# Hybrid S5 and sparse-attention block: factors of B ahead of the last tables, octet 0's rotation products behind the next weights, the second sweep's spills on SyncE

## The chip, the cores and the metric

One core of one Trainium2 chip. The time is that of one execution on the device in microseconds (us); before the change it is 2343.06, the median of 3 runs (2338.4 to 2365.14). The engines are TensorE (PE), VectorE (DVE), ScalarE (ACT), GpSimd (POOL) and SyncE (SP). Each executes its own instructions in the order of its queue; a transfer (DMA) is issued by an engine, here SP or POOL, and carried by the 16 transfer engines of the core.

## The reference

A decoder block on x (1, 512, 2048). An adaLN-modulated RMSNorm feeds one combined projection; its output goes to a diagonal complex state-space group (S5, 64 groups of 16 channels with 64 states) and to sparse attention, whose keys and values are some of the projection's columns. A convolutional gated MLP follows.

```python
h = modulate(rmsnorm(x, g_mix_norm[l]), sh1, sc1)
u, q, kc, vc, ks, vs, kw, vw, gl = jnp.split(h @ w_in[l], split_at, axis=-1)
...
den = lr * lr + li * li                    # in s5_mixer
f_re = (num_re * lr + ab_im * li) / den
f_im = (ab_im * lr - num_re * li) / den
bb_re = f_re[..., None] * br - f_im[..., None] * bi
bu = lax.complex(jnp.einsum('bsgh,gph->sbgp', uf, bb_re), jnp.einsum('bsgh,gph->sbgp', uf, bb_im))
_, states = lax.associative_scan(_lin_rec_combine, (a, bu), axis=0)
y = (einsum(real(states), c_re) - einsum(imag(states), c_im) + d_skip * uf)
```

## The kernel before, in words

**Precision.** Each float32 operand of a large product is split in two: ACT rounds a copy (`..h`), DVE subtracts it from the source (`..l`; `split`, L72 to L78, which a profile shows as L75). A product is three matmuls of 128x128 on 128x512 (`mm3`, L100 to L102); only the third reads the low half of the weight.

**Phase a** (`phase_a`, L211) runs twice over the 16 blocks of D. The second sweep fills eight PSUM banks: four heads of keys `pk[0..3]`, four blocks of values. At its end the first bank is rotated (`rope`), each is split into a buffer `adw` and written to DRAM, keys to `qk_d` (`spill`, L675, two halves of 512 rows, 512 KB each), values to `v_d` (L319, 256 KB each), for the attention later. All eight transfers are issued by POOL.

**S5 tables** (`s5_prep`, L339) are made by POOL at low priority during phase a: powers of the state matrix (PR, PI), a table of rotations in two factors (CA, SA and CB, SB; from CA, SA the copies CH, SH), and the factors of B, `s5fr` and `s5fi` (fr, fi), one of whose inputs is a reciprocal on DVE (L441). It is a generator, called at the start and the end of the first sweep. Its last stage normalises both tables (L485 to L491).

**Phase b1** (`phase_b1`, L677) has 12 projections of 48 matmuls. `weights` (L80) loads 1 MB (`wr`, two buffers, SP) and splits it in two halves (`wh`, `wl`, two buffers each). Projection 0 is followed by a rope on DVE (L708 to L710, `qt`, `qr`), whose tables `rt` (a tile of name `sp`) SP loads at L685. Between the projections stand the eight octets of S5 (`s5_octet`, L508). On DVE an octet forms `s5bb` = B with fr and fi (L526 to L532), `s5bg` from it (L542 to L544, transposed by PE at L585), `s5TT` (L547), the six rotation products `s5C`, `s5S` (L563 to L569; C and S are later copied and scaled by ACT), and, later, the bias row `s5wt` (L610), which reads `shb`, a broadcast of the shift, loaded behind the values' spills by POOL (L689). The block matrix goes out to `k_s` and back into the single buffer `s5w3` (shown as `s5w`, L603). The tiles of the octets lie in memory that phase a's buffers, `adw` among them, held.

**Order.** The code is in program order; a scheduler at build time orders each engine's queue by its estimates of when operands are ready, and by priority (`tc.high_priority`, with a negative number for late). `self.after(parts, x)` keeps instructions behind x, on the engine's queue or by a wait; `Held(V, f)` is an engine that does so with each instruction that it is given.

Of the kernel before, what the change touches and what calls it, by code (L numbers as in the profile page):

```python
# [10 lines left out]
F32 = mybir.dt.float32  # L11
# [3 lines left out]
ALU = mybir.AluOpType  # L15
# [3 lines left out]
P = 128  # L19
D = 2048  # L20
# [44 lines left out]
class Block:  # L65
    def __init__(self, ctx, tc, a):
        self.ctx, self.tc, self.a = ctx, tc, a
        self.nc = tc.nc
        self.V, self.A, self.T = tc.nc.vector, tc.nc.scalar, tc.nc.tensor


    def split(self, src, hi, lo, scale=None):  # L72
# [7 lines left out]
    def weights(self, src, out=None, first=None):  # L80

        res = []
        with self.tc.high_priority():
            raw = self.wp.tile([P, 2048], F32, name="wr", bufs=2)
            self.nc.sync.dma_start(raw, src)
            for h in range(2):
                if out is None:
                    hi = self.wp.tile([P, 8, P], F32R, name="wh", bufs=2)
                    lo = self.wp.tile([P, 8, P], F32R, name="wl", bufs=2)
                else:  # L90
                    hi, lo = out[:, 2 * h], out[:, 2 * h + 1]
                parts = self.split(raw[:, 1024 * h:1024 * h + 1024].rearrange("p (k m) -> p k m", m=P), hi, lo)
                if first is not None:
                    self.after(parts, first)
                res.append((hi, lo))
        return res

# [113 lines left out]
    def phase_a(self, hh, hl, tab, ps):  # L211


        nc, tc, a, V, A, T = self.nc, self.tc, self.a, self.V, self.A, self.T
        m, b = self.mod, self.mad
        with ExitStack() as st:
            pa = st.enter_context(tc.tile_pool(name="pa", bufs=1))
            pw = st.enter_context(tc.tile_pool(name="pw", bufs=1, side="right"))
            xq = [pa.tile([P, 4, S], F32, name=f"x{q}") for q in range(4)]
            xt = [xq[k // 4][:, k % 4] for k in range(KT)]  # L220
            rb = pa.tile([P, S], F32, name="rb")
# [54 lines left out]
            for kt in range(KT):  # L276
# [3 lines left out]
                V.tensor_add(m[:, 0, kt:kt + 1], ash, b[:, 0, kt:kt + 1])  # L280
                if kt >= 8:
                    hl[kt] = tab.tile([P, S], F32R, name=f"hl{kt}")
                self.modulate(xt[kt], m[:, 1, kt:kt + 1], m[:, 0, kt:kt + 1], rb, hh[kt], hl[kt], pa)
                if kt < 8:
                    V.tensor_mul(us[kt], us[kt], rp)
                if kt == 4:
# [20 lines left out]
            for i in range(4):  # L307
                p = pk[i]
                if i == 0:
                    q, t = (pa.tile([P, 8, 64], F32, name="modt", bufs=2).rearrange("p a b -> p (a b)")  # L310
                            for _ in range(2))
                    p = self.rope(p, q, t, self.rot[:, 0], self.rot[:, 1], 64)
                if i % 2 == 0:
                    o = tmp(4).bitcast(F32R)
                self.spill(self.qk_d[0, P * i:P * i + P], p, o[:, 2 * (i % 2):2 * (i % 2) + 2])
            o = tmp(4)
            for t in range(4):
                A.copy(o[:, t], pk[4 + t])
                self.v_spill = nc.gpsimd.dma_start(self.v_d[t], o[:, t])  # L319

    def modulate(self, x, gain, shift, rb, hi, lo, pool, t=None):
        if t is None:
# [16 lines left out]
    def s5_prep(self, pool, W):  # L339
# [4 lines left out]
        with tc.high_priority(-100000):  # L344
            n = [0]

            def t(shape=(P, 64), dt=F32, name=None):
                n[0] += 1
                return W.tile(list(shape), dt, name=name or f"sp{n[0]}")
# [83 lines left out]
        with tc.high_priority(-100000):  # L433
# [4 lines left out]
            V.tensor_mul(den, lr, lr)  # L438
            V.tensor_mul(q, li, li)
            V.tensor_add(den, den, q)  # L440
            self.V.reciprocal(rd, den)  # L441
            V.tensor_scalar(nr, ar, -1.0, None, op0=ALU.add)
            fr = pool.tile([P, 64], F32, name="s5fr")
            fi = pool.tile([P, 64], F32, name="s5fi")
            V.tensor_mul(fr, nr, lr)
            V.tensor_mul(q, ai, li)
            V.tensor_add(fr, fr, q)
            V.tensor_mul(fr, fr, rd)
            V.tensor_mul(fi, ai, lr)
            V.tensor_mul(q, nr, li)  # L450
            V.tensor_sub(fi, fi, q)
            V.tensor_mul(fi, fi, rd)
            V.tensor_scalar(fi, fi, sgn, None, op0=ALU.mult)
            r8 = pool.tile([P, 64], F32, name="s5r8")
            V.tensor_mul(r8, mag, mag)
            V.tensor_mul(r8, r8, r8)
# [25 lines left out]
            cmul(fc, fs, ec, es, ec, es, tmp[:, 0])  # L482
            powers(CA, SA, fc, fs)
            n1 = t((P, 8, 64))
            for C, Sn in ((CB, SB), (CA, SA)):  # L485

                V.tensor_mul(n1, C, C)
                V.tensor_mul(tmp, Sn, Sn)
                V.tensor_add(n1, n1, tmp)
                V.tensor_scalar(n1, n1, -0.5, 1.5, op0=ALU.mult, op1=ALU.add)  # L490
                V.tensor_mul(C, C, n1)  # L491
                V.tensor_mul(Sn, Sn, n1)
                V.tensor_scalar(Sn, Sn, sgn, None, op0=ALU.mult)
# [14 lines left out]
    def s5_octet(self, o, Tb, W, ps):  # L508
# [49 lines left out]
            return tab[:, :, G].rearrange("p b g -> p g b").unsqueeze(2).to_broadcast([P, 8, 4, 8])  # L558


        Ch, Sh = C[:, :, 0:4], Sn[:, :, 0:4]
        tc1 = W.tile([P, 8, 8, 8], F32, name="s5x", bufs=4)[:, :, 0:4]
        V.tensor_mul(Ch, ab(Tb["CH"]), ba(Tb["CB"]))  # L563
# [3 lines left out]
        V.tensor_mul(Sh, ab(Tb["SH"]), ba(Tb["CB"]))  # L567
        V.tensor_mul(tc2, ab(Tb["CH"]), ba(Tb["SB"]))
        V.tensor_add(Sh, Sh, tc2)  # L569
        for x, sg in ((C, 1.0), (Sn, -1.0)):  # L570
            A.activation(x[0:64, :, 4:8], x[64:P, :, 0:4], AF.Copy, scale=sg)
            A.copy(x[64:P, :, 4:8], x[64:P, :, 0:4])
            A.activation(x[64:P, :, 0:4], x[0:64, :, 0:4], AF.Copy, scale=sg)
# [96 lines left out]
        V.tensor_add(q, q, t)  # L670
        return q

    def spill(self, dst, q, t, scale=None):
        self.split(q, t[:, 0], t[:, 1], scale)
        self.nc.gpsimd.dma_start(dst, t.bitcast(F32))  # L675

    def phase_b1(self, hh, hl):  # L677
        nc, tc, a, V, A, T = self.nc, self.tc, self.a, self.V, self.A, self.T
        with ExitStack() as st:
# [6 lines left out]

            nc.sync.dma_start(self.sh_d.rearrange("o (p k) -> (o p) k", k=KT), self.mod[:, 0])
            shb = self.shb = W.tile([P, D], F32, name="shb")
            self.after([nc.gpsimd.dma_start(shb, self.sh_d.to_broadcast([P, D]))], self.v_spill)  # L689
            n = 0  # L690

            def octet(n):
# [846 lines left out]
```

## Time and profile before

| | us |
|---|---|
| median of 3 runs (2365.14, 2343.06, 2338.4) | 2343.06 |
| the profiled execution's own time | 2354.09 |
| its span, first to last instruction | 2352.3 |
| PE, DVE, ACT, POOL busy | 2195.6, 1854.9, 1080.2, 309.6 |
| mean granted clock of PE, share of full speed | 0.967 |

The rows further down are from the trace of this one execution; times in them run from the start of the span. A name as `wl` stands for all tiles of that name. What stands in brackets behind an instruction is how long its engine was idle before it, and who released it.

### The profile page before, as it was taken

What the parts mean: (1) busy time and instruction counts of PE and PEld (TensorE: products, weight loads), DVE (VectorE), ACT (ScalarE), POOL (GpSimd) and SP (SyncE); (2) the same over time, 40 slices, a digit from 0 to 9 for tenths busy, and PEclk for the clock granted to TensorE, in tenths of its full rate; (3) what the DMA queues carried; (4) which work ended last, traced back from release to release, by engine and by line L of the source; (5) the groups of instructions that cost most, each with busy time, mean ns of one, the idle gap of its engine ahead of it and who ended that gap; (6) DMA issues with size and microseconds to landing.
All of it is one profiled execution on the core that took longest, in us unless ns stands there. A gap on an engine that the chain in (4) does not pass through costs nothing.

```text
span 2352.3 us, 34734 instructions
## 1 busy us (share of the span) xinstructions
PE 2195.6 (93%) x13694; PEld 1918.0 (82%) x13694; DVE 1854.9 (79%) x2776; ACT 1080.2 (46%) x1823; POOL 309.6 (13%) x376
## 2 busy tenths in 40 slices
PE   7997899878899878899999999999999999999997
PEld 5776778666677666899999999999999788888886
DVE  7896888658988877889999999999999773553436
ACT  3422444348867742744445444454444431221215
POOL 8999111100000011000000000000000000000000
PEclk9999999979999989999999999999999999999998
DMA  9784656576477467233333333333333783443223
GB/s 345 289 284 177 207 167 177 158 209 207 150 239 228 171 258 287 85 123 127 126 129 126 122 122 122 122 121 122 122 121 112 286 310 120 148 145 119 90 90 108
DMA packets 94003, 398.20 MB, mean 169 GB/s; under 512 B 19968, under 2 KB 28448, under 8 KB 58384
## 3 DMA queue, kind: packets, MB, share of 16 engines
q1 hardware_dynamic: 79440, 344.51, 42.0%
q0 software_dynamic: 14400, 51.49, 6.6%
q8 instruction: 107, 1.75, 0.3%
q14 instruction: 56, 0.46, 0.1%
HBM read 358.20 MB, written 37.69 MB: 168 GB/s over the span
## 4 chain that ended last, share of the span: by engine, by line
PE 54%; issue 4%; DVE 3%; ACT 1%; DMA 1%; POOL 1%; POOLq 0%; DVEq 0%; ACTq 0%
PE dn L102 7%; PE dn L100 7%; PE dn L101 6%; PE sa L101 6%; PE sa L100 6%; PE sa L102 6%; PE sb L100 5%; PE sb L102 5%; PE sb L101 5%; DMA adw<-in_wada_dram 0%; DVE wl L75 0%; DMA a_d<-cv 0%; POOL adw L119 0%; POOL x_d L1045 0%; DVE cv L1090 0%
## 5 line engine op out<-in xcount | busy, mean ns | idle before, releaser
L75 ACT CAST wh<-wr 128x1024 fp32r<-128x1024 f32 (+1 forms) x257 | 262.0, 1024 | 502.5 <-PE dn L101 320.5
L75 DVE TENSOR_TENSOR wl<-wr,wh 128x1024 fp32r<-128x1024 f32 (+1 forms) x255 | 307.6, 1210 | 50.1 <-ACT wh L75 38.8
L124 DVE SCALAR_TENSOR_TENSOR adw<-adw,silc 128x2048 f32<-128x2048 f32 x63 | 146.7, 2331 | 26.4 <-DMA adw<-in_wada_dram 25.3
L100 PE MATMUL mm<-yh,wh 128*128 128x512 f32 (+1 forms) x320 | 129.4, 409 | 26.7 <-DVE x L1043 7.8
L75 ACT CAST xh<-wq 128x1024 fp32r<-128x1024 f32 x84 | 88.3, 1052 | 139.2 <-DVE wq L1229 104.2
L75 ACT CAST wh<-wq 128x1024 fp32r<-128x1024 f32 x84 | 88.3, 1052 | 137.8 <-DVE wq L1229 104.5
L1099 POOL DMA_DIRECT2D a_d<-cv x44 | 23.8, 541 | 856.5 <-DVE cv L1098 856.5
L101 PE MATMUL mm<-yl,wh 128*128 128x512 f32 (+1 forms) x320 | 128.8, 403 | 7.4 <-DVE yl L75 7.4
L102 PE MATMUL mm<-yh,wl 128*128 128x512 f32 (+1 forms) x320 | 127.9, 401 | 1.9 <-DVE wl L75 1.9
L1293 DVE SCALAR_TENSOR_TENSOR x<-dn,mod,x 128x512 f32<-128x512 f32 (+1 forms) x56 | 37.6, 673 | 108.3 <-PE dn L102 107.8
L75 DVE TENSOR_TENSOR xl<-wq,xh 128x1024 fp32r<-128x1024 f32 x84 | 102.4, 1218 | 24.2 <-ACT xh L75 24.2
L75 DVE TENSOR_TENSOR wl<-wq,wh 128x1024 fp32r<-128x1024 f32 x84 | 102.2, 1218 | 22.7 <-ACT wh L75 22.7
L100 PE MATMUL dn<-b21h,wh 128*128 128x512 f32 x256 | 101.8, 398 | 3.1 <-ACT wh L75 3.1
L102 PE MATMUL dn<-b21h,wl 128*128 128x512 f32 x256 | 102.1, 399 | 0.5 <-DVE wl L75 0.5
L1229 DVE TENSOR_TENSOR wq<-wq,wr 128x1024 f32<-128x1024 f32 x84 | 102.0, 1215 | 0.1
L101 PE MATMUL dn<-b21l,wh 128*128 128x512 f32 x256 | 101.8, 398 | 0.0
L100 PE MATMUL dn<-t4h,wh 128*128 128x512 f32 (+1 forms) x256 | 97.8, 382 | 0.0
L102 PE MATMUL dn<-t4h,wl 128*128 128x512 f32 (+1 forms) x256 | 97.7, 382 | 0.0
L101 PE MATMUL dn<-t4l,wh 128*128 128x512 f32 (+1 forms) x256 | 97.6, 381 | 0.0
L100 PEld LDWEIGHTS mm<-yh,wh 128*128 128x128 f32 x320 | 62.7, 198 | 41.7 <-issue 16.9
L146 POOL TENSOR_TENSOR rms_r<-rms_v,mhalf 128x2 f32<-128x2 f32 (+1 forms) x8 | 10.8, 1346 | 637.5 <-DVE rms_v L144 637.4
L102 PE MATMUL mm<-hh,wl 128*128 128x512 f32 x192 | 79.5, 414 | 15.9 <-DVE wl L75 15.9
(535 smaller groups left out, 7852.8 us busy)
## 6 DMA issues: line engine op xcount, KB each, us to landing
adw<-in_wada_dram SPq DMA_DIRECT2D x49, 1024.0 KB, 6.7
wr<-in_wup_dram SPq DMA_DIRECT2D x46, 1024.0 KB, 4.9
wq<-in_wup_dram SPq DMA_DIRECT2D x42, 1024.0 KB, 6.8
wr<-in_wdn_dram SPq DMA_DIRECT2D x40, 1024.0 KB, 4.9
wr<-in_wada_dram SPq DMA_DIRECT2D x32, 1024.0 KB, 4.9
wr<-in_wout_dram SPq DMA_DIRECT2D x16, 1024.0 KB, 5.5
adw<-in_wada_dram POOLq DMA_DIRECT2D x14, 1024.0 KB, 7.7
wr<-in_wp_dram SPq DMA_DIRECT2D x12, 1024.0 KB, 5.2
```

The source lines that it names most:

```text
L75: return self.A.copy(hi, src), self.V.tensor_sub(lo, src, hi.bitcast(F32))
L100: self.T.matmul(ps, wh, xh, start=start, stop=False)
L101: self.T.matmul(ps, wh, xl, start=False, stop=False)
L102: self.T.matmul(ps, wl, xh, start=False, stop=stop)
L124: self.V.scalar_tensor_tensor(t, t, 1.0, self.silc, op0=ALU.mult, op1=ALU.mult, accum_out=out)
L146: self.rms_pow = self.nc.gpsimd.tensor_tensor(r[:, 0:n], v[:, 0:n], self.mhalf.to_broadcast([P, n]), op=ALU.pow)
L1099: self.nc.gpsimd.dma_start(self.a_d[:, m], val)
L1229: V.tensor_add(src, src, add)
L1293: V.scalar_tensor_tensor(x, p, gate, x, op0=ALU.mult, op1=ALU.add)
```

## The change

1. In `s5_prep` the reciprocal and the three multiplications that finish fr and fi leave the middle of the tables and stand at the head of a third stage, which is entered at block 8 of the second sweep. The reciprocal is held behind that block's modulation on DVE. The normalisation of the tables is held behind the last of the three.
2. The six rotation products of octet 0 are held on DVE behind `self.lo[-2]`, a low half of the latest weights that have been emitted.
3. The eight spills of the second sweep and the load of `shb` are issued by SP.

```diff
@@ weights
                 if first is not None:
                     self.after(parts, first)
+                self.lo.append(parts[1])
                 res.append((hi, lo))
@@ phase_a, second sweep
-                self.modulate(xt[kt], m[:, 1, kt:kt + 1], m[:, 0, kt:kt + 1], rb, hh[kt], hl[kt], pa)
+                self.modulated = self.modulate(xt[kt], m[:, 1, kt:kt + 1], m[:, 0, kt:kt + 1], rb, hh[kt], hl[kt], pa)
+                if kt == 8:
+                    next(prep)
...
-                self.spill(self.qk_d[0, P * i:P * i + P], p, o[:, 2 * (i % 2):2 * (i % 2) + 2])
+                self.spill(self.qk_d[0, P * i:P * i + P], p, o[:, 2 * (i % 2):2 * (i % 2) + 2], queue=nc.sync)
             o = tmp(4)
             for t in range(4):
                 A.copy(o[:, t], pk[4 + t])
-                self.v_spill = nc.gpsimd.dma_start(self.v_d[t], o[:, t])
+                nc.sync.dma_start(self.v_d[t], o[:, t])
@@ s5_prep
-            self.V.reciprocal(rd, den)
...
-            V.tensor_mul(fr, fr, rd)
...
-            V.tensor_mul(fi, fi, rd)
-            V.tensor_scalar(fi, fi, sgn, None, op0=ALU.mult)
...
             n1 = t((P, 8, 64))
+        yield
+        with tc.high_priority(-100000):
+            with tc.high_priority(200000):
+                self.after([self.V.reciprocal(rd, den)], self.modulated)
+            V.tensor_mul(fr, fr, rd)
+            V.tensor_mul(fi, fi, rd)
+            last = V.tensor_scalar(fi, fi, sgn, None, op0=ALU.mult)
+            V = Held(V, lambda i: self.after([i], last))
             for C, Sn in ((CB, SB), (CA, SA)):
@@ s5_octet
+        if o == 0:
+
+            lo = self.lo[-2]
+            V = Held(V, lambda i: self.after([i], lo))
         Ch, Sh = C[:, :, 0:4], Sn[:, :, 0:4]
...
         V.tensor_add(Sh, Sh, tc2)
+        V = self.V
@@ spill
-    def spill(self, dst, q, t, scale=None):
+    def spill(self, dst, q, t, scale=None, queue=None):
         self.split(q, t[:, 0], t[:, 1], scale)
-        self.nc.gpsimd.dma_start(dst, t.bitcast(F32))
+        (queue or self.nc.gpsimd).dma_start(dst, t.bitcast(F32))
@@ phase_b1
-            self.after([nc.gpsimd.dma_start(shb, self.sh_d.to_broadcast([P, D]))], self.v_spill)
+            nc.sync.dma_start(shb, self.sh_d.to_broadcast([P, D]))
```

VectorE's queue before, from projection 0's second `wl` over the last splits of the sweep (`adw`) to octet 0; the `wl` in the ninth row is the first half of projection 1:

```order
L75 TENSOR_TENSOR wl<-wr,wh 128x1024
L75 TENSOR_TENSOR adw<-b,adw 128x512 x2
L516 MEMSET s5SS 128x8
L563 TENSOR_TENSOR s5C<-s5CH,s5CB 128x8x32
L564 TENSOR_TENSOR s5x<-s5SH,s5SB 128x8x32
L567 TENSOR_TENSOR s5S<-s5SH,s5CB 128x8x32
L565 TENSOR_TENSOR s5C<-s5C,s5x 128x8x32
L568 TENSOR_TENSOR s5x<-s5CH,s5SB 128x8x32
L75 TENSOR_TENSOR wl<-wr,wh 128x1024
L526 TENSOR_TENSOR s5bb<-s5bc,s5fr 128x128
L527 TENSOR_TENSOR s5tb<-s5bc,s5fi 128x128
L526 TENSOR_TENSOR s5bb<-s5bc,s5fr 128x128
```

The same place after the change:

```order
L76 TENSOR_TENSOR wl<-wr,wh 128x1024
L76 TENSOR_TENSOR adw<-b,adw 128x512 x2
L76 TENSOR_TENSOR wl<-wr,wh 128x1024
L524 MEMSET s5SS 128x8
L721 TENSOR_TENSOR qt<-mm,sp 32x512
L722 TENSOR_TENSOR qr<-mm,sp 32x512
L76 TENSOR_TENSOR wl<-wr,wh 128x1024
L723 TENSOR_TENSOR qr<-qr,qt 32x512
L721 TENSOR_TENSOR qt<-mm,sp 32x512
L722 TENSOR_TENSOR qr<-mm,sp 32x512
L534 TENSOR_TENSOR s5bb<-s5bc,s5fr 128x128
```

The rotation products are no longer here (they stand behind the second `wl` of projection 2, which is the second one after these rows). The first and second `wl` of projection 1 are rows 3 and 7, and between them stand two instructions of projection 0's rope, which read `sp`, the table `rt`.

SyncE's queue before, from the load of projection 1's weights to the loads of octet 0 and of its `s5wt`:

```order
L85 DMA wr<-in_wp_dram 128x2048
L685 DMA sp<-in_rt_dram 128x1024
L85 DMA wr<-in_wp_dram 128x2048
L503 DMA s5bc<-in_s5bc_dram 128x512
L505 DMA s5U<-u_d 128x512
L597 DMA s5dd<-in_s5d_dram 16x128
L609 DMA s5wt<-in_wuT_dram 128x1024
```

And after; the second `wr` is projection 2's in both:

```order
L86 DMA wr<-in_wp_dram 128x2048
L688 DMA qk_d<-adw 128x1024 x2
L86 DMA wr<-in_wp_dram 128x2048
L688 DMA qk_d<-adw 128x1024 x2
L323 DMA v_d<-adw 128x512 x4
L698 DMA sp<-in_rt_dram 128x1024
L702 DMA shb<-sh_d 128x2048
L511 DMA s5bc<-in_s5bc_dram 128x512
L513 DMA s5U<-u_d 128x512
```

The spills stand ahead of the load of `rt`, and `shb` behind it. In PE's queue octet 0's transposes (L585, now L598) move from 29 matmuls into projection 1 to 8 into projection 2, and octet 5's last product from the end of projection 10 to 0.4 of projection 11; further on the queues come to the same order.

## Rows read from the trace of the kernel before

**Rows 1.** The page of the profile: span and number of instructions, the busy time of the engines (with share of the span and number of instructions), and what the transfers moved in each of 40 equal slices of the span.
```profile
span 2352.3 us, 34734 instructions
...
PE 2195.6 (93%) x13694; PEld 1918.0 (82%) x13694; DVE 1854.9 (79%) x2776; ACT 1080.2 (46%) x1823; POOL 309.6 (13%) x376
...
GB/s 345 289 284 177 207 167 177 158 209 207 150 239 228 171 258 287 85 123 127 126 129 126 122 122 122 122 121 122 122 121 112 286 310 120 148 145 119 90 90 108
```

**Rows 2.** The list of TensorE's waits over the whole span, grouped by line: who waited, for whom; us in total, times, the longest.
```profile
PE mm L102 <- DVE wl L75: 17.8, 3, 15.9
...
PE acc L647 <- DMA s5w<-k_s: 7.9, 1, 7.9
...
PE acc L638 <- DVE bu L613: 2.7, 1, 2.7
```

**Rows 3.** TensorE's timeline where projection 0 ends and projection 1 begins: start in us, duration in us, engine, line, operation, tiles and shape, and in brackets the idle time before and what ended it.
```profile
222.43 0.39 PE L100 MATMUL mm<-hh,wh 128*128 128x512 f32 x1
222.66 0.39 PE L101 MATMUL mm<-hl,wh 128*128 128x512 f32 x1
238.98 0.79 PE L102 MATMUL mm<-hh,wl 128*128 128x512 f32 x1 [15.93 <-DVE wl L75]
239.57 0.63 PE L100 MATMUL mm<-hh,wh 128*128 128x512 f32 x1
...
244.69 0.40 PE L100 MATMUL mm<-hh,wh 128*128 128x512 f32 x1
```

**Rows 4.** Windows of the span: stretch and its length, busy us (and instructions) of each engine, the granted clock of TensorE as a share of full speed, the busy share of the transfer engines, GB/s. The last row is from a second answer.
```profile
core 0: us, PE busy (x) PEld busy (x) DVE busy (x) ACT busy (x) POOL busy (x), PEclk, DMA share, GB/s
...
224.00:238.90 14.90, 0.00 (x0) 0.00 (x0) 3.69 (x7) 2.08 (x5) 11.73 (x19) 0.62 0.44 165
238.90:245.00 6.10, 6.02 (x15) 4.72 (x16) 6.07 (x14) 1.39 (x2) 0.80 (x3) 0.53 0.96 322
245.00:262.00 17.00, 16.10 (x82) 12.78 (x81) 16.60 (x28) 6.75 (x12) 1.63 (x3) 1.00 0.67 236
...
280.40:286.00 5.60, 5.60 (x35) 4.48 (x36) 5.53 (x12) 3.47 (x10) 0.00 (x0) 1.00 0.26 91
```

**Rows 5.** VectorE's timeline from the last splits of the second sweep to octet 0 (columns as in rows 3).
```profile
214.00 1.62 DVE L75 TENSOR_TENSOR wl<-wr,wh 128x1024 fp32r<-128x1024 f32 x1
...
229.58 0.60 DVE L563 TENSOR_TENSOR s5C<-s5CH,s5CB 128x256 f32<-128x256 f32 x1 [12.74 <-POOL s5SH L59]
235.82 0.61 DVE L564 TENSOR_TENSOR s5x<-s5SH,s5SB 128x256 f32<-128x256 f32 x1 [5.63 <-DMA qk_d<-adw]
...
237.71 1.21 DVE L75 TENSOR_TENSOR wl<-wr,wh 128x1024 fp32r<-128x1024 f32 x1
238.84 0.28 DVE L526 TENSOR_TENSOR s5bb<-s5bc,s5fr 128x128 f32<-128x128 f32 x1
...
240.45 1.21 DVE L542 TENSOR_TENSOR s5bg<-s5bb,s5PR 128x1024 f32<-128x1024 f32 x1
...
242.81 0.69 DVE L708 TENSOR_TENSOR qt<-mm,sp 32x512 f32<-32x512 f32 x1
...
250.46 1.35 DVE L547 TENSOR_TENSOR s5TT<-s5bc,s5PR 128x1152 f32<-128x1152 f32 x1
...
254.62 1.21 DVE L610 SCALAR_TENSOR_TENSOR s5wt<-s5wt,shb 128x1024 f32<-128x1024 f32 x1
```

**Rows 6.** GpSimd's timeline: one of the last table stage, the factors of B, and the first and the last transfers issued by it there.
```profile
219.12 1.57 POOL L59 TENSOR_SCALAR s5SB<-s5SB,cons 128x512 f32<-128x512 f32 x1
...
229.63 0.74 POOL L59 TENSOR_TENSOR s5fr<-s5fr,sp 128x64 f32<-128x64 f32 x1
...
231.13 1.21 POOL L675 DMA_DIRECT2D qk_d<-adw  x2
...
235.52 0.55 POOL L689 DMA_DIRECT2D shb<-sh_d  x1
```

**Rows 7.** ScalarE's timeline: the high half of projection 1's first weights.
```profile
217.01 1.05 ACT L75 CAST wh<-wr 128x1024 fp32r<-128x1024 f32 x1
```

**Rows 8.** SyncE's queue: two transfers that it issued (start, us to issue), and its longest wait from 198 to 262 (columns as in rows 2).
```profile
203.34 0.42 SPq L685 DMA_DIRECT2D sp<-in_rt_dram  x1
...
242.41 0.34 SPq L597 DMA_DIRECT2D s5dd<-in_s5d_dram  x1
...
SPq L597 <- DMA v_d<-adw: 25.4, 1, 25.4
```

**Rows 9.** Transfers issued from 195 to 262: tiles, queue, times, KB each (of 1024 bytes), median us from issue to landing.
```profile
wr<-in_wp_dram SPq DMA_DIRECT2D x5, 1024.0 KB, 4.9
qk_d<-adw POOLq DMA_DIRECT2D x4, 512.0 KB, 4.5
...
v_d<-adw POOLq DMA_DIRECT2D x4, 256.0 KB, 6.4
shb<-sh_d POOLq DMA_DIRECT2D x1, 1024.0 KB, 10.4
...
sp<-in_rt_dram SPq DMA_DIRECT2D x1, 512.0 KB, 5.6
```

**Rows 10.** GpSimd's queue late in the projections: the output of octet 5 and the load of octet 6's block matrix.
```profile
422.96 1.28 POOL L652 DMA_DIRECT2D z_d<-s5x  x1 [14.06 <-ACT s5x L651]
...
446.48 1.33 POOL L603 DMA_DIRECT2D s5w<-k_s  x1 [7.03 <-DMA k_s<-s5bg]
```

More of the change, by code (lines that the diff above doesn't have):

```diff
@@ L69, in __init__ @@
         self.V, self.A, self.T = tc.nc.vector, tc.nc.scalar, tc.nc.tensor
+        self.lo = []
     def split(self, src, hi, lo, scale=None):
```

## The prediction

> **What bounds the kernel now.** I read the busy times of the page first: TensorE (PE) is busy 2195.6 of 2352.3 us [rows 1], so a gain must come from its idle time or its clock. Next the list of PE's waits, grouped by line: of 17.8 us in which a product `mm` waits for the low half of a weight, `wl`, 15.9 are one single wait [rows 2]. PE's timeline then places it: the two first matmuls of projection 1 start at 222.43 and 222.66, the third, the first that reads `wl`, at 238.98 [rows 3]. The windows show the rest of the price: PE does nothing from 224 to 238.9, and in the 6 us behind it the granted clock is 0.53, the lower of the two levels (1.2 instead of 2.4 GHz), where the stretch from 245 has 1.00 [rows 4].
>
> Why is `wl` late? VectorE (DVE) executes in order. The weight half had its high part from ScalarE (ACT) at 217.01+1.05 = 218.06 [rows 7]. But ahead of that `wl` stand five of octet 0's six rotation products: the first, at 229.58, waits 12.74 us, from 216.8 on, for GpSimd (POOL) to copy the tables, the second another 5.63 us for the spill `qk_d` of the second sweep, whose buffer holds the memory that it writes; `wl` itself starts at 237.71 and takes 1.21 [rows 5]. The spills are that late because they stand on POOL's queue behind the last table, and go out at 231.13 to 235.5 [rows 6]. So one chain, POOL's tables to spills to DVE to PE, stops the kernel once; it is not a rate that bounds.
>
> **What the change removes.** The rotation products move behind the second half of projection 2's weights, so `wl` of projection 1 stands straight behind the last splits of the sweep: 218.06 plus 1.21, done at 219.3, and PE wants it at 222.66+0.23 = 222.9. It is free 3.6 us before it is wanted. Removed: 15.9 of idle, and the low clock behind it. From 239.57 to 244.69 are 12 intervals of matmuls, 5.12 us; at the 0.23 between the two ahead of the gap [rows 3] they would take 2.76. That is 2.4, together 18.3 us.
>
> **What it adds.** (a) *A wait for `rt`.* The load of the rope tables `rt` (tile `sp`), issued at 203.34 before, long ahead of its use, now stands on SyncE's (SP's) queue behind four `qk_d` and four `v_d`. DVE's next instruction behind `wl` is the rope of projection 0 (`qt<-mm,sp`), and it waits for `rt`; queued behind it is the second `wl` of projection 1, and PE waits for that. Bytes ahead, and its own: 4 x 0.524 (`qk_d`) + 1.05 (a `wr` load, between them) + 4 x 0.262 (`v_d`) + 0.524 = 4.72 MB [rows 9]. The first spill can go when the split that fills it ends, about 214.1, where DVE turns to the `wl` at 214.00 [rows 5]. The nearest row for a backlog on the transfer engines is the window 238.9 to 245 with 322 GB/s [rows 4]: 14.7 us, `rt` lands at 228.8. Bounds: 345 GB/s, the first slice of the page [rows 1], gives 227.8; the same spills before, 3.15 MB from 231.13 to the release of SP at 242.41 [rows 6, 8], are 279 GB/s and give 231.0. I take 228.8, because the new stretch mixes loads and spills as that window does.
> Then DVE does two rope products of 0.69 and `wl` of 1.21 [rows 5]: done 231.4. PE wants it 24 matmuls after 222.9, at 228.4. New idle: 3.0 us (2.0 to 5.2).
>
> (b) *Octet 0 on DVE without a gap to hide in.* Before, its small products ran while PE caught up. Now, from 231.4, DVE has four more rope products (0.69), six small ones on B and C (0.2 each: eight fill 238.84 to 240.45 [rows 5]) and `wl` of projection 2, 1.21: done 236.6. PE, resumed at 231.4, is through projection 1 after 22 intervals at 236.5 and wants that `wl` at 236.9: no wait, but with 0.3 in hand only (0 to 1.3, the small load `s5bc` arriving a little late included). Behind it stand one small product, two products of 1.21, one of `TT` of 1.35 and the sum of 1.21 [rows 5]: `s5bg` done at about 241.6. PE's transposes of it stand 8 matmuls into projection 2 now, at 236.5+1.8 = 238.3. New idle: 3.3 us (0 to 5).
>
> (c) *Factors of B earlier.* The same reciprocal and three small POOL instructions, 1.5 us in all [rows 6], run ahead of the last table stage instead of behind it; the tables end when they ended before, at about 231, since POOL's amount is the same. The rotation products that want them come at about 244 now: 13 us of cover. Without that cover DVE would wait for the tables as before. `fr` and `fi` are ready at about 212, and first read after 231. Nothing.
>
> (d) *SP issues nine transfers more, POOL nine fewer.* Some 0.4 us each on SP, 3.6 in all. It had a single wait of 25.4 us there [rows 8], which covers them. `shb`, which took 10.4 us behind the spills [rows 9], is read first at 254.62 [rows 5]; behind the same bytes and its own 1.05 MB it lands 3 us after `rt`, at 232. Nothing.
>
> (e) *Clock after the new gaps.* Behind the gap of 15.9 the low clock cost 2.4; behind octet 0's wait of 2.7 at L638 [rows 2], which ends at 280.4, the clock is 1.00 [rows 4]. So 0 to 2.4 for each new gap, 0 to 4.8. I take 0: gaps of 3 us are nearest to the 2.7.
>
> (f) *Octet 0's own wait before*, the 2.7 at L638 [rows 2], may go, since its place has slid back: a gain of 0 to 2.7. I take 0: what it waits for on DVE slides back as far.
>
> **Sum.** 18.3 - 3.0 - 3.3 = 12.0 us. Behind the projections the queues stand in the same order as before, so what is won at 245 is kept unless octets turn into the bound. The profiled execution took 2354.09; 2342.1 by that. It lies 11.0 above the median of the three runs (2343.06), so the forecast is 2331.
>
> **One rule against it.** The `wl` at 214.00, with POOL at work beside it, took 1.62; the one at 237.71, with POOL idle, 1.21 [rows 5, 6]. So a neighbour on POOL costs some 0.4 us, which I left out since it falls on the first `wl`, with 3.6 us in hand. The Trainium skill (SBUF — State Buffer, "Who interferes with whom") says more: a DVE instruction with two inputs in SBUF and a GpSimd instruction that reads SBUF exclude each other for the whole instruction. The trace here shows the smaller loss only. The sum by the rule is under the rivals.
>
> **Rivals.** *Octets become the bound and give it back.* Octet 0's transposes stand 0.6 of a projection further back in PE's order, some 6 us, and octet 5's output, at 422.96 on POOL's queue, 0.4 of one. The single buffer of `s5w` for octet 6 is loaded at 446.48 after octet 5 has read it, and PE waits for that load 7.9 us [rows 2, 10]. It delays that load only if octet 5 ends more than 446.48 - 422.96 = 23.5 less the 1.3 of issue later than before, and the order moves it by about 5. Against it. If DVE, and not PE, sets the pace of octets 1 to 5, the gain of 12 shrinks to 0 to 5: 2340.
> *More waits vanish.* With (f) in full, (a) and (b) at their lower bounds, and the tail's 7.9 gone too, the gain is 18.3 - 2.0 + 2.7 + 7.9 = 27, the time 2316. For it speaks that octet 6's part of the chain is 12 us earlier; against it that PE is earlier by the same 12.
> *POOL locks DVE out.* A POOL instruction of up to 1.57 [rows 6] holds the second `wl`, at 230.2 while the tables still run, and PE 1.6 longer: gain 10.4, 2333. This is the outcome by the rule of the page above; the 0.4 of the rows speaks against it.
> *Slower: the spills crawl, and `rt` with them.* Everything as in (a), but if spills and loads on one queue moved at half of 279 GB/s, `rt` lands at 248, PE idles 22, and 18.3 - 22 - 3.3 = -7: 2354.09 + 7 - 11 = 2350. It decides when `rt` lands later than 240.8 (3.0 + 12.0 of idle), a mean of 177 GB/s from 214.1. The windows with a backlog speak against it (322).
> *The change does nothing*: 2343. It would need another late input of the first `wl`; the trace has none, ACT's half is there at 218.06.
>
> **Chances.** Forecast as summed 0.58; bound by octets 0.16; more waits vanish 0.14; POOL's lock 0.06; nothing 0.03; spills crawl 0.03. About 1% (23 us) is what a measurement of this kernel can tell from no change, so under 2319.6 counts as faster and over 2366.5 as slower. Of the forecast's own range, 2324 to 2340 ((a), (b), (e), (f) at their bounds: 18.3 - 2.0 + 2.7 = 19.0, and 18.3 - 5.2 - 5 - 4.8 = 3.3), nothing is past either; most of the rival with 2316 is: faster 0.13. Slower by over 23 us takes a landing after 264: 0.02. The rest, 0.85, is within 1%. The range of 8 in 10 goes from 2315, about the fast rival's time, to 2346: the 2343 of no effect and some 3 us for the spread of medians (the two lowest runs lie 4.7 apart). It leaves out the slow rival and the outer part of the fast one.
>
> **What would show it.** In the profile of the changed kernel: no wait of PE at L102 (L104 by its new number) over 5 us near 223 to 240; a granted clock of 1.00 there; `rt` landing near 228.8, as the release of the first `qt`; a wait of PE for a second `wl` of about 3 us, then one for `s5bg` at the transposes of about 3 us; tables ending near 231 and the rotation products starting after 240 without waiting for POOL. The prediction is wrong if `rt` lands after 235, if PE waits for octets 1 to 7 more than before, or if the wait at `s5w` grows by what was won.

## The result and the profile after

The change makes the kernel 0.67% faster: the ratio is 0.9933, with a 95% interval of 0.9918 to 0.9949. The medians of 16 runs each are 2333.96 us after and 2348.09 before (the three runs of before that stand above had 2343.06). The forecast was 2331, in a range that holds the result. It stood on the median of three runs; taken from the median of 16, the forecast gain of 12.0 would have given 2336. Of the profiled executions, that of after took 2333.46 us, close to its median; that of before, 2354.09, lies 6 above the median of 16.

The page after, as in [rows 1], shows the same work in a shorter span:

```profile
span 2331.7 us, 34742 instructions
...
PE 2197.5 (94%) x13694; PEld 1916.5 (82%) x13694; DVE 1855.0 (80%) x2776; ACT 1080.3 (46%) x1823; POOL 307.6 (13%) x367
```

The stage that the change touches is measured from the first matmul of projection 0 to the first product with the values in the attention, `pv`. First the kernel before, then after (TensorE's timeline):

```profile
211.55 0.39 PE L100 MATMUL mm<-hh,wh 128*128 128x512 f32 x1
...
530.21 0.50 PE L913 MATMUL pv<-tch,vc 64*128 64x512 f32 x1
```
```profile
210.81 0.39 PE L102 MATMUL mm<-hh,wh 128*128 128x512 f32 x1
...
516.76 0.49 PE L926 MATMUL pv<-tch,vc 64*128 64x512 f32 x1
```

That is 318.7 us before and 305.9 after: 12.8 won, where the sum of the prediction had 12.0. These are single executions: a second one of the changed kernel took 302.1 for the stage (all_parts below), so differences under some 4 us between stages say little, and that the two numbers agree to 0.8 is in part luck. TensorE's list of waits, to hold against [rows 2]:

```profile
PE mm L104 <- DVE wl L76: 4.5, 3, 3.8
...
PE tp L598 <- DVE s5bg L552: 3.9, 2, 3.3
...
PE acc L660 <- DMA s5w<-k_s: 2.5, 1, 2.5
```

VectorE's timeline, to hold against [rows 5], with the load of `rt` on SyncE and its landing in the list of transfers, which answer to [rows 8, 9]:

```profile
217.35 1.95 DVE L76 TENSOR_TENSOR wl<-wr,wh 128x1024 fp32r<-128x1024 f32 x1 [0.67 <-ACT wh L76]
...
229.01 0.68 DVE L721 TENSOR_TENSOR qt<-mm,sp 32x512 f32<-32x512 f32 x1 [9.68 <-DMA sp<-in_rt_dram]
...
230.32 1.20 DVE L76 TENSOR_TENSOR wl<-wr,wh 128x1024 fp32r<-128x1024 f32 x1
...
233.75 0.29 DVE L534 TENSOR_TENSOR s5bb<-s5bc,s5fr 128x128 f32<-128x128 f32 x1
...
236.01 1.22 DVE L76 TENSOR_TENSOR wl<-wr,wh 128x1024 fp32r<-128x1024 f32 x1
...
240.88 1.22 DVE L552 TENSOR_TENSOR s5bg<-s5bg 128x1024 f32<-128x1024 f32 x1
...
244.42 0.62 DVE L59 TENSOR_TENSOR s5C<-s5CH,s5CB 128x256 f32<-128x256 f32 x1
```
```profile
219.78 0.83 SPq L698 DMA_DIRECT2D sp<-in_rt_dram  x1
```
```profile
sp<-in_rt_dram SPq DMA_DIRECT2D x1, 512.0 KB, 9.1
```

The first `wl` of projection 1 is done at 219.3, as forecast. `rt` is issued at 219.78 and lands 9.1 later, at 228.9 (228.8 in the prediction). The second `wl` is done at 231.5 (231.4), projection 2's first at 237.2 (236.6), `s5bg` at 242.1 (241.6). The first rotation product starts at 244.42 with no wait for GpSimd, whose tables end at 233.0. TensorE's timeline, to hold against [rows 3], and its windows, against [rows 4]:

```profile
227.36 0.39 PE L103 MATMUL mm<-hl,wh 128*128 128x512 f32 x1
231.58 0.79 PE L104 MATMUL mm<-hh,wl 128*128 128x512 f32 x1 [3.83 <-DVE wl L76]
232.17 0.63 PE L102 MATMUL mm<-hh,wh 128*128 128x512 f32 x1
...
237.72 0.40 PE L103 MATMUL mm<-hl,wh 128*128 128x512 f32 x1
...
242.15 1.09 PE L598 MATMUL tp<-cons,s5bg 128*128 128x128 f32 x8 [0.61 <-DVE s5bg L552]
```
```profile
230.00:236.00 6.00, 4.42 (x10) 3.47 (x11) 5.88 (x13) 2.20 (x3) 4.42 (x7) 0.57 0.90 332
```
```profile
440.00:450.00 10.00, 7.50 (x26) 3.98 (x24) 6.12 (x9) 0.57 (x1) 0.00 (x0) 0.50 0.60 172
450.00:460.00 10.00, 10.00 (x36) 7.28 (x35) 3.77 (x11) 3.71 (x8) 2.96 (x3) 0.52 0.26 77
```

The wait of 15.93 is one of 3.83. But behind it the clock is low again: from 232.17 to 237.72 are 13 intervals, 5.55 us where 2.96 would do at 0.2275. It costs 2.6, and it lets VectorE catch up, so the wait at the transposes is 0.61 and not 3.3. The head of the stage loses 3.8 + 2.6 + 0.6 = 7.0 us; the prediction had 3.0 + 3.3 = 6.3.

Behind the head one wait of octet 0 remains, about as long as the 2.7 of [rows 2]. There the clock stayed at 1.00; here 10.2 us at half speed follow the wait, some 5 us lost, which the prediction did not have (the second execution, below, has neither the wait nor the stretch):

```profile
276.24 0.43 PE L661 MATMUL acc<-s5SS,s5TT 128*128 128x64 f32 x2 [2.65 <-DVE s5SS L656]
```
```profile
278.70:288.90 10.20, 10.20 (x39) 9.23 (x39) 5.72 (x10) 5.39 (x11) 2.62 (x2) 0.50 0.62 171
```

The two windows ahead of these, from 440 to 460, show what was not foreseen either: TensorE runs at 1.2 GHz for 20 us, where the kernel before had some 10 (a granted clock of 0.51 from 450 to 460). What stands ahead of that, and in it, is idle time at octets 6 and 7 (the list of TensorE's waits from 425 to 483, and VectorE's timeline ahead of the first of them):

```profile
PE tp L598 <- DVE s5bg L552: 3.3, 1, 3.3
PE acc L660 <- DMA s5w<-k_s: 2.5, 1, 2.5
...
PE acc L651 <- DVE s5x L648: 1.2, 1, 1.2
```
```profile
435.19 0.69 DVE L646 TENSOR_TENSOR s5x<-s5x,s5S 128x512 f32<-128x512 f32 x1 [2.14 <-DMA z_d<-s5x]
```

TensorE waits 3.3 for octet 7's `s5bg`; VectorE makes it late because the instruction ahead waits 2.14 for octet 5's output to leave one of the four buffers `s5x`.

### The profile page after: what moved, and what is told of

Read it like the earlier page. It is cut to its first block, busy times and chain, and to the rows that moved or that the text cites. A ratio compares the mean times of both kernels' runs of the same rounds, so it can differ in the third digit from the quotient of the medians.

```text
span 2331.7 us, 34742 instructions
## 1 busy us (share of the span) xinstructions
PE 2197.5 (94%) x13694; PEld 1916.5 (82%) x13694; DVE 1855.0 (80%) x2776; ACT 1080.3 (46%) x1823; POOL 307.6 (13%) x367
## 4 chain that ended last, share of the span: by engine, by line
PE 71%; DVE 13%; issue 7%; DMA 4%; ACT 4%; POOL 1%; SPq 0%; POOLq 0%; DVEq 0%; ACTq 0%
PE sa L104 7%; PE sa L103 7%; PE sa L102 7%; PE dn L104 6%; PE dn L102 6%; PE dn L103 6%; PE sb L102 5%; PE sb L104 5%; PE sb L103 5%; PE mm L102 2%; PE mm L103 2%; DVE wl L76 2%; PE mm L104 2%; PE b L103 1%; PE s L900 1%
## 5 line engine op out<-in xcount | busy, mean ns | idle before, releaser
L76 ACT CAST wh<-wr 128x1024 fp32r<-128x1024 f32 (+1 forms) x257 | 261.9, 1024 | 496.2 <-PE dn L103 320.5
L1300 DVE TENSOR_TENSOR x<-x,dn 128x512 f32<-128x512 f32 x32 | 22.0, 686 | 91.5 <-PE dn L104 91.5
```

Source lines behind the costliest of these rows:

```text
L76: return self.A.copy(hi, src), self.V.tensor_sub(lo, src, hi.bitcast(F32))
L1300: V.tensor_add(x, x, p)
```

## The experiments

The table gives median, ratio to the kernel before with its interval, and the stage as above, from one profiled execution each. The last column counts in TensorE's timeline how many of the 32 matmuls of the gate (a small product that follows the last projection, `gate` in the kernel) start ahead of octet 6's last product; the tail takes it up. The stage of zz_gate_late is not to be held against the others: 19 more matmuls of the next product (1424 instead of 1405) start inside it.

| run | median us | ratio | stage us | gate ahead |
|---|---|---|---|---|
| kernel before | 2348 to 2351 | 1 | 318.7 | 0 |
| the whole change (all_parts) | 2333.87 | 0.9935 [0.9916, 0.9954] | 305.9, 302.1 | 0 |
| spills_only | 2327.99 | 0.9912 [0.9888, 0.9935] | 299.7 | 14 |
| hold_only | 2340.88 | 0.9967 [0.9952, 0.9982] | 309.8 | 0 |
| no_factors | 2335.56 | 0.9944 [0.9923, 0.9966] | 305.1 | 0 |
| shb_first | 2331.93 | 0.9926 [0.9897, 0.9955] | 295.4 | 3 |
| rt_first | 2332.26 | 0.9922 [0.9903, 0.9940] | 302.1 | 0 |
| zz_in_u | 2320.89 | 0.9870 [0.9850, 0.9890] | 282.9 | 21 |
| zz_again (the same) | 2316.66 | 0.9861 [0.9835, 0.9887] | 284.8 | 21 |
| rt_zz | 2316.62 | 0.9864 [0.9843, 0.9884] | 289.6 | 21 |
| before_zz | 2347.92 | 0.9987 [0.9969, 1.0005] | 320.9 | 0 |
| spills_zz | 2334.23 | 0.9927 [0.9903, 0.9952] | 302.4 | 0 |
| zz_gate_late | 2325.74 | 0.9897 [0.9874, 0.9920] | 301.2 | 0 |

### The parts

**Spills alone**, on the kernel before (with the argument of `spill`):

```diff
-                self.v_spill = nc.gpsimd.dma_start(self.v_d[t], o[:, t])
+                nc.sync.dma_start(self.v_d[t], o[:, t])
...
-            self.after([nc.gpsimd.dma_start(shb, self.sh_d.to_broadcast([P, D]))], self.v_spill)
+            nc.sync.dma_start(shb, self.sh_d.to_broadcast([P, D]))
```

> The spills and the broadcast of the shift go out by SyncE; no hold of the rotation products, factors of B where they were. Theory (two blocks in series, tables and then spills, stood before the first low half of projection 1, and only the second of them is gone): that low half now stands ahead of the rotation products and is free, but the products of two octets stand ahead of the second low half and still wait for GpSimd's tables until about 229.6; nine of them at 0.5 us, two rope products and the split end at about 236.6, and TensorE wants it at 228.4: a wait of about 8 and about 2.5 lost at the low clock, where the kernel before has 18.3. Gain 7 to 8 us against the kernel before, half of the whole change. Rival 1 (moving the spills is all that counts): gain 14 to 16. Rival 2 (moving them is worth nothing without the hold): within 2 us of the kernel before.

Measured: 0.9912, a gain of some 20 us: more than even rival 1's 14 to 16, and by its interval no less than the whole change. VectorE's and TensorE's timelines:

```profile
216.90 2.37 DVE L75 TENSOR_TENSOR wl<-wr,wh 128x1024 fp32r<-128x1024 f32 x1 [0.24 <-ACT wh L75]
...
231.01 0.59 DVE L563 TENSOR_TENSOR s5C<-s5CH,s5CB 128x256 f32<-128x256 f32 x1 [11.72 <-POOL s5SH L59]
...
235.19 0.69 DVE L708 TENSOR_TENSOR qt<-mm,sp 32x512 f32<-32x512 f32 x1
...
236.63 1.22 DVE L75 TENSOR_TENSOR wl<-wr,wh 128x1024 fp32r<-128x1024 f32 x1
```
```profile
236.65 0.79 PE L100 MATMUL mm<-hh,wh 128*128 128x512 f32 x1 [9.81 <-ACT wh L75]
```
```profile
440.00:450.00 10.00, 10.00 (x62) 7.66 (x62) 6.14 (x15) 3.85 (x9) 2.96 (x3) 1.00 0.78 230
450.00:460.00 10.00, 9.53 (x51) 8.60 (x50) 2.76 (x5) 6.33 (x15) 0.00 (x0) 1.00 1.06 208
```

The head is as expected: the first `wl` needs no hold to stand ahead of the rotation products, since the scheduler places it there by itself once the spills are on SyncE; the products wait 11.72 for the tables, and TensorE idles 9.8 for projection 1's second half (for its high part, which stands on ACT behind the copies of the rotation products; `wl` is no earlier, done at 237.8). With 2.2 at the transposes and some 1.4 of low clock the head loses 6 us more than with the whole change. But from 440 to 460 the clock is 1.00, and from 425 to 460 TensorE waits nowhere for more than 0.5 us; a slow stretch comes only behind that (0.60 from 460 to 470, 0.50 from 470 to 490). So the theory has the head, and the tail made up the difference. What differs there is the order: 14 of the gate's matmuls start ahead of octet 6's last product, which is the second of these rows, and none does in the whole change.

```profile
435.84 0.39 PE L745 MATMUL mm<-hh,wh 128*128 128x512 f32 x1
...
445.74 0.39 PE L648 MATMUL acc<-s5SS,s5TT 128*128 128x64 f32 x2
```

**The hold alone**, on the kernel before:

```diff
+                self.lo.append(parts[1])
...
+        if o == 0:
+            lo = self.lo[-2]
+            V = Held(V, lambda i: self.after([i], lo))
```

> Only octet 0's rotation products are held behind the later weights; spills stay on GpSimd, factors of B stay behind the tables. Theory: the first low half of projection 1 is free at 219.3, but behind it octet 0's products with the factors of B stand ahead of the rope and of the second low half. The factors come at 230.3 to 231.1 and the buffers may wait for the late spills until 236; the second low half ends at 237 to 241, where TensorE wants it at 228.4: a wait of 8.5 to 12.6 and 2.5 of low clock. Gain 3 to 7 us against the kernel before. Rival (the hold is the whole change): gain 14 to 16.

Measured: 0.9967, a gain of 8 us (0.33% of 2350), a little over the 3 to 7. As expected, the products with the factors of B stand ahead of the second `wl`, and TensorE waits for that:

```profile
231.28 0.39 DVE L528 TENSOR_TENSOR s5bb<-s5bc,s5fr 128x128 f32<-128x128 f32 x1 [13.40 <-POOL s5fr L59]
```
```profile
238.44 0.80 PE L104 MATMUL mm<-hh,wl 128*128 128x512 f32 x1 [11.52 <-DVE wl L76]
```

The stage is 8.9 us shorter. The hold is not the whole change.

**Without the factors**: both diffs together, `s5_prep` as before.

> The change without its first part: spills on SyncE and the hold, factors of B at the end of the tables as before. Theory: the factors end at about 231 and VectorE reads them first at 233.7, since it waits for the rope's table until 229, so this part is worth 0: ratio to the kernel before as for the whole change, 0.992 to 0.995 (gain 13 to 17 us). Rival (the factors are late once the rest is quick): the first product on B waits for GpSimd 1 to 5 us, and the gain shrinks by that.

Measured: 0.9944; its interval holds the whole change's 0.9933. The first product on B started at 233.42 and waited for nothing. This part is worth nothing that can be told beside the other two.

The run also sets the spills and the hold together beside the spills alone, on the same chip: 2335.56 (2329.1 to 2342.5, 8 runs) against 2327.99 (2323.3 to 2332.1, 6 runs). So the hold, worth 8 us by itself, costs some 8 once the spills are on SyncE. TensorE's waits in the head fall by it, from 9.8 and 2.2 to 4.6 and 0.7, and the loss lies further on, where the gate's matmuls go from 14 ahead to none.

### The wait for `rt`

**More bytes ahead of it.** In `phase_b1`:

```diff
-            nc.sync.dma_start(rt, a["rt"])
...
             nc.sync.dma_start(shb, self.sh_d.to_broadcast([P, D]))
+            nc.sync.dma_start(rt, a["rt"])
```

> The whole change, but on SyncE's queue the broadcast of the shift (1.05 MB) and octet 0's two small loads (0.52 MB) stand ahead of the load of the rope's table instead of behind it. Theory (that load lands when the bytes ahead of it and its own have been moved, at 322 to 415 GB/s): it lands 3.8 to 4.9 us later, at 232.7 to 233.8 instead of 228.9, and TensorE's wait for the second low half grows from 3.8 to 7.6 to 8.7; the time grows by about 4 us against the whole change (2338 where that has 2334). Rival (the load is late for its own issue or its own length, not for the bytes ahead): it lands within 1.5 us of 228.9 plus what its issue moved, and the time stays within 1 us of the whole change.

SyncE's timeline and the landing; TensorE's wait:

```profile
225.06 0.33 SPq L702 DMA_DIRECT2D sp<-in_rt_dram  x1
```
```profile
sp<-in_rt_dram SPq DMA_DIRECT2D x1, 512.0 KB, 8.8
```
```profile
238.19 0.50 PE L102 MATMUL mm<-hh,wh 128*128 128x512 f32 x1 [4.58 <-ACT qr L724]
```

`rt` lands at 225.06 + 8.8 = 233.9, 5 us later, as the theory of the bytes ahead has it. The time did not follow: 2331.93. The scheduler put the second `wl` ahead of the rope on VectorE, and TensorE's wait moved to the start of projection 2 (4.58, where it needs the accumulator that the rope reads). So the landing was right. Its price was not tested as it was meant to be: a late load costs what stands behind its reader in the queue, and the queue was sorted anew.

**`rt` ahead of the spills.** The load is emitted at high priority:

```diff
-            nc.sync.dma_start(rt, a["rt"])
+            with tc.high_priority(4000):
+                nc.sync.dma_start(rt, a["rt"])
```

> The whole change, with the load of the rope's table at high priority: on SyncE's queue it stands behind the first spill instead of all eight; the queues of the other engines are the same, row for row. Theory (that load sets the 3.8 us wait for the second low half and the 2.6 of low clock behind it): it lands before 220, the second low half is done at about 225.5 and TensorE, which wants it at 227.6, does not wait. Octet 0's transposes are then reached at 234.5, and the products before them end at about 237.8, held by octet 0's load of B: a wait of 3.3, with or without a slow clock behind it. The head of the stage loses 3.3 to 5.9 where the whole change loses 7.0: 1 to 4 us faster than the whole change if the tail of the projections keeps it. Rival 1 (the octets' tail sets the end of the stage): the wait is gone, the time within 1 us of the whole change or longer. Rival 2 (the gain of the head is kept whole): 6 to 7 us faster.

```profile
222.35 0.69 DVE L722 TENSOR_TENSOR qt<-mm,sp 32x512 f32<-32x512 f32 x1 [2.55 <-PE mm L104]
...
232.42 0.29 DVE L534 TENSOR_TENSOR s5bb<-s5bc,s5fr 128x128 f32<-128x128 f32 x1 [4.47 <-DMA s5bc<-in_s5bc_dram]
```
```profile
236.03 0.50 PE L104 MATMUL mm<-hh,wl 128*128 128x512 f32 x1 [2.38 <-DVE wl L76]
...
240.90 1.78 PE L598 MATMUL tp<-cons,s5bg 128*128 128x128 f32 x8 [3.21 <-DVE s5bg L552]
```

The rope starts at 222.35 and the wait for the second `wl` is gone. Now the next load is late: `s5bc`, behind the spills, lets VectorE go on at 232.42, and TensorE waits 2.38 and 3.21 instead. 2332.26 beside 2333.87 for the whole change on the same chip: 1.6 us less, in the theory's 1 to 4, but the runs of the two overlap, so that rival 1 (no gain) is not excluded. The 3.21 is the theory's second wait (3.3); the 2.38 it did not have. TensorE's waits in the head come to 4.4 in the whole change (3.83 and 0.61), to 5.7 in its second execution (1.10, 2.11 and 2.45), to 6.0 in shb_first and to 5.6 here: they move from load to load and do not go away.

> The whole change once more, on the chip and in the rounds of the three kernels beside it. Theory and rival alike: ratio 0.992 to 0.995 against the kernel before.

It was 0.9935. In the profiled execution `rt` was issued at 216.44 and landed at 225.0, 3.9 us earlier than in the first execution of the same kernel.

### The tail

**Outputs over the input tiles.** In `s5_octet`, for the whole change:

```diff
-            zz = W.tile([P, 8, 64], F32, name="s5x", bufs=4)
+            zz = U
```

> The whole change, with each octet's output written over its input tile instead of into the four buffers of the octet's temporaries. The scheduler moves octets 2 to 6 by up to 0.5 of a projection. Theory (in the tail VectorE waits 2.1 us for an octet's output to leave such a buffer, and TensorE waits 3.3 for the products behind it; the idle time is followed by 20 us at the low clock): both waits go, and the time falls by 3 to 10 us against the whole change. Rival (the tail waits for the order of octets 5 to 7 and not for a buffer): the wait moves to another of the octet's products, the time stays within 2 us of the whole change.

Measured: 0.9870, 13 us under the whole change on the same chip and more than the theory's 3 to 10. It was run once more beside the last three kernels below:

> The whole change with the outputs over the input tiles, once more on the chip of the three beside it: 2317 to 2324 by either theory.

That gave 0.9861. The stage is 283 to 285 instead of 302 to 306. But two things changed: the buffer, and the order, in which 16 of the gate's 32 matmuls (not 33, as an expectation below has it) now stand ahead of octet 6's last products, and 5 more among them, and not behind them. Both together with `rt` first:

> Both of the two before: the rope's table loaded behind the first spill, outputs written over the input tiles. Theory (head and tail lose separately): the two gains add, 4 to 14 us faster than the whole change. Rival (one bound, the octets): no faster than the better of the two.

It was 2316.62: 17 us under the whole change on the same chip, more than the theory's 4 to 14, and 4.3 under the edit by itself there (2320.89). But the edit by itself gave 2316.66 in its second run, and the ratios (0.9864 beside 0.9870 and 0.9861) do not differ. So loading `rt` first is not shown to add anything, as the rival had it.

**Which of the two?**

> The kernel before, with each octet's output written over its input tile (the edit that made the changed kernel 13 us faster). VectorE does not wait there for an octet's output to leave a buffer, and octet 6's last products stand ahead of the gate's matmuls in TensorE's queue, before and with the edit. Theory (what the edit gains exists only behind the change, where octets 5 to 7 come later against TensorE): within 4 us of the kernel before. Rival (the edit gains by itself): 8 to 14 us faster than the kernel before.

Measured: 0.9987, nothing. The edit gains only behind the change; here it leaves the gate's matmuls where they are, all behind octet 6.

> Only the spills and the broadcast by SyncE (as in the run of that alone, 2328), with the outputs written over the input tiles. Octet 6's last products stand ahead of the gate's matmuls here. Buffer theory (the gain of the edit is the wait for the outputs to leave the shared buffers): another 5 to 13 us faster than the spills alone, 2315 to 2323. Order theory (the gain is that the gate's matmuls stand ahead of octet 6's last products and fill TensorE while VectorE finishes that octet): no gain, 2325 to 2333 or more.

Measured: 2334.23, no gain over the spills alone on that chip (2327.99). That is the order theory's outcome, but no clean test of the buffer: the edit also took the gate's matmuls from 14 ahead to none, and a gain from the buffer may hide behind that loss. The third holds the gate back:

```diff
+            if o == 6:
+                self.y6 = y
...
+            if not k:
+                self.after([y], self.y6)
```

> The whole change with the outputs over the input tiles, and the first matmul of the gate held on TensorE behind octet 6's last product. Before octet 6's gate the order is that of the run without the hold; behind it the gate's 33 matmuls, 16 of which stood ahead of octet 6's last products, stand behind them. Order theory: TensorE idles and then runs at the low clock at the end of the projections again, and most of the 13 us are lost: 2329 to 2336. Buffer theory: the time stays at 2318 to 2324.

TensorE's list of waits at the end of the projections, without the hold (zz_in_u) and with it, and the windows of both:

```profile
PE acc L660 <- DMA s5w<-k_s: 4.6, 1, 4.6
...
PE acc L651 <- DVE bu L626: 1.4, 1, 1.4
```
```profile
PE acc L651 <- DVE bu L626: 7.0, 1, 7.0
```
```profile
430.00:440.00 10.00, 7.82 (x38) 5.00 (x38) 8.32 (x17) 2.08 (x8) 0.56 (x1) 1.00 0.87 282
440.00:450.00 10.00, 10.00 (x69) 9.06 (x68) 5.93 (x12) 7.43 (x17) 2.65 (x2) 1.00 1.07 230
```
```profile
430.00:440.00 10.00, 4.37 (x14) 3.24 (x14) 6.09 (x12) 2.18 (x9) 0.23 (x1) 0.51 0.35 142
440.00:450.00 10.00, 10.00 (x44) 9.35 (x44) 1.38 (x5) 4.84 (x10) 1.68 (x2) 0.50 0.00 0
```

The wait at octet 6 grows from 1.4 to 7.0, and the granted clock is 0.50 until 450, where without the hold it is 1.00 from 420 to 450 (0.91 to 1.00 in zz_again). The time is 2325.74, 9.1 above the run without the hold on the same chip (2316.66). That lies between the two forecasts, 2329 to 2336 and 2318 to 2324, so neither theory holds alone. Nor does the hold give back just the order of the whole change: it also leaves 12 of the gate's matmuls behind octet 7's first product, where every other kernel has none.

So the gate's place is shown to matter, by 9.1 us in this kernel, of the 13 to 17 that the edit gained; whether the rest (some 8 us to the whole change's 2333.9) is the buffer or the places of octets 2 to 5 stays open. The last column of the table points the same way, though it is a comparison and not an experiment: of the kernels with the spills on SyncE, those with 0 or 3 matmuls ahead took 2332 to 2336 (zz_gate_late alone 2326), the one with 14 took 2328, those with 21 took 2317 to 2321. It is also the likeliest reason why the spills alone did better than the whole change.

## Why the prediction came out

- *What is removed* (18.3) held in the amount: the wait of 15.9 and the slow stretch behind it are gone (the slow stretch that is left stands behind the 3.83 and belongs to (e)). The cause that the prediction gave, the rotation products' hold, does clear the first `wl` by itself, but so do the spills by themselves. Either alone leaves TensorE waiting for the second half of the weights, 11.5 with the hold and 9.8 with the spills; only both together bring that to 3.8.
- *(a) `rt`*: landing 228.9 for 228.8, wait 3.8 for 3.0. That bytes ahead set the landing is borne out by shb_first. The hit to 0.1 is luck: the first spill went at 210.6 and not at 214.1; from 214.1 to the landing the transfers moved 336 GB/s instead of 322, part of it for loads issued behind `rt`; and in the second execution `rt` landed at 225.0. The price attached to it (each us of landing is a us of TensorE) was wrong, as rt_first shows: landed at 215.6, it gained 1.6 us.
- *(b) Octet 0*: `s5bg` at 242.1 for 241.6 (the prediction's own terms add to 241.8); the wait was 0.6 for 3.3, since TensorE was slower on the way there.
- *(c), (d)*: (c) is nothing, as forecast (no_factors). (d) was not tried by itself; the load of `rt` took 0.83 us to issue, twice the 0.42 of [rows 8].
- *(e) Clock*: taken as 0, it was 2.6 in the head and some 5 behind octet 0's wait of 2.65. The row of 2.7 idle with the clock at 1.00 carried over neither to 3.8 idle nor to 2.65. In the head the 2.6 cancelled (b), so the sum there was 7.0 for 6.3: the parts were off, the sum was not, since both take the same time.
- *(f) and the tail*: octet 0's wait of 2.7 at L638 is gone, but one of 2.65 stands at its next products (L661), so the 0 came out, without its clock. The wait at `s5w` fell from 7.9 to 2.5, not kept and not grown. In its place came octet 7's 3.3 and twice as long a stretch at the low clock. "Behind the projections the queues stand in the same order as before, so what is won at 245 is kept" was true as a sum (12.8 of 12.0), not as a mechanism: over the stage TensorE's idle time fell by 19.2 us (46.6 to 27.4), and its busy time, for the same 1405 matmuls, rose by 6.5 (272.1 to 278.6). Waits shrank and the low clock took part of that back.
- *Rival, octets become the bound*: half right. It named the single buffer `s5w`, where 2.5 us were lost; the larger loss lies with octet 6's last products, which stand ahead of work that could have filled TensorE, as far as the runs on the gate show it.
- *POOL's lock*: weighed wrongly, though it cost nothing here. VectorE's and GpSimd's timelines where the first `wl` of projection 1 is made, after the change and in no_factors:

```profile
216.93 1.29 POOL L59 TENSOR_TENSOR s5CB<-s5CB,sp 128x512 f32<-128x512 f32 x1
```
```profile
216.26 1.23 DVE L76 TENSOR_TENSOR wl<-wr,wh 128x1024 fp32r<-128x1024 f32 x1 [0.22 <-ACT wh L76]
```
```profile
216.29 2.35 POOL L59 TENSOR_TENSOR s5CB<-s5CB,sp 128x512 f32<-128x512 f32 x1
```

After the change GpSimd is first (216.93 to 218.22): `wl`, begun at 217.35, takes 1.95 and ends 1.08 behind it, about its own 1.21. In no_factors VectorE is first by 0.03: `wl` takes 1.23 and GpSimd's product 2.35 instead of 1.29. So one waits for nearly the whole of the other. That is what the Trainium skill has (SBUF — State Buffer, "Who interferes with whom"). The 0.4 that the prediction read from one pair of rows was a part of an overlap, and the trace of before held the rest of it: GpSimd's product at 214.52, next to that `wl`, took 2.00, and its like at 220.65 took 1.04. In the changed kernel the first `wl` still ended at 219.3, 2.9 ahead of the matmul that reads it (222.15). The second, at 230.32, took 1.20, as if alone; GpSimd's copy beside it took 2.02, and the one at 227.77 took 0.39.

Not settled: the spans of the two profiled executions differ by 20.6 us, the stage by 12.8. The rest lies behind that stage, where the change touches nothing, and the medians differ by 14.1; the execution of before was a long one. Behind the stage the profiled executions of the fourteen runs take 1814 to 1824 us, whatever the edit; before (1822) and after (1815) lie in that range.

## What to carry to other kernels

When a stall goes, price what is next as one amount for the stretch, not wait by wait: loads, splits and the clock behind a gap trade places. Undo each part alone before crediting it; here one of three did at least as much as all, since another, a gain by itself, became a loss beside it. Where a scheduler orders the queues, compare them first: an edit of a buffer moved half of the gate's matmuls. And look at the end of the stage too: where a chain on another engine finishes there, independent work that stands behind its last products in TensorE's queue belongs ahead of them; the edit that did so here, and took away a buffer with it, gave the best times of all (2317 to 2321).

## What the runs showed of the hardware

Gaps of similar length are not followed by the same clock. Behind 3.8 us of idle time came 13 intervals at half speed. Behind 2.7 at octet 0 in the kernel before came none, behind 2.65 at octet 0 in the changed kernel 10.2 us. In the second execution of the changed kernel a slow stretch began behind idle times of 1.1 and 2.1, at 236.1, and lasted to 246.4. At the end of the projections, idle times of 3.3 and 1.2, and one of 2.5 inside it, went with 20 us at half speed (439.4 to 459.6): some 9 us lost, more than the 7.0 of idle time itself. A late operand and a slow clock cost less together than one by one, since TensorE at half speed asks later for what is late: at the transposes it waited 0.6 where 3.3 was forecast.
